# Strassen's scheme for 17 of the 22 weight pairs of the first FFN product

## The chip, the cores and the metric

One core of one Trainium2 chip. The metric is the time of one execution on the device, in microseconds (us); a kernel is run several times and the median is compared. TensorE (PE) multiplies, VectorE (DVE), ScalarE (ACT) and GpSimd (POOL) do elementwise work, SyncE (SP) issues the transfers.

## What is computed

One encoder block on 512 tokens of width 1024 (16 learned meta tokens are put in front for attention). Two attention mixers are merged and added to the stream; then comes the feed-forward part, with which the change has to do:

```python
u = rms_norm(h, pre_ffn_gain[l])
gate_up = u @ w_ffn_in[l]                      # (512, 1024) @ (1024, 2 * 2816)
f = (jax.nn.silu(gate_up[..., :D_FF]) * gate_up[..., D_FF:]) @ w_ffn_out[l]
h = h + rms_norm(f, post_ffn_gain[l])
```

All data are float32. The kernel writes each operand of a product as the sum of a high and a low part in a reduced float32 format (`float32r`) and replaces one product by three: high times high, high times low, low times high.

## The kernel before

Everything is one function, `encoder`. Its stages run one after the other on PE: projections and attention, the merge, the out-projection (`m_out`), normalization and transposition of the tokens (`m_norm`), FFN-in, FFN-out. The order of PE's instructions is the program's order, written by hand and, between out-projection, transposes and FFN-in, by a small planner (`Order`, run in line 1181), in which each piece has a cost and a time at which it is due. The order of the instructions of DVE, ACT, POOL and SP is settled at compile time: roughly, of the instructions whose operands and buffers are available, the one that stands first in the program goes first. On the chip each engine then takes its instructions in that fixed order. Buffers are tiles of pools; all tiles with the same tag share that tag's slots, and a new tile waits until the last reader of an old one is done.

Split (`split`, lines 255 to 261; `sub_hi`, line 252): ACT casts a tile to the high part, DVE subtracts it from the source for the low part. `load_w` (lines 265 to 279) loads 128 x 1024 weights (tag `wr`, three slots), casts them on ACT (line 271) and subtracts on DVE; for the loads number 4 to 51 POOL subtracts three quarters of it (lines 274 to 278, both recorded at line 252). `mm3` (lines 283 to 288) issues the three matmuls.

`m_norm` (lines 1117 to 1153) normalizes the four groups t of 128 tokens, transposes each on PE (line 1147) and splits the result into `uh` and `ul`, 8 blocks of 128 features by 512 tokens (lines 1148 to 1151).

FFN-in (`ffn_in`, lines 1169 to 1179): for each of 22 pairs j of a gate tile and an up tile, 128 output columns each, `proj_g` runs 8 blocks k of `mm3`, first for gate, then for up; ACT takes Silu of gate, DVE multiplies it by up and the product `sg` is split into the hidden tile j (`hid`, tags `xh`, `xl`, `hy0`, `hy1`). The first three pairs run twice, on token columns 0 to 255 and 256 to 511, the other 19 once on all 512 (lines 1110 to 1115):

```python
for c0, c1 in ((0, 256), (256, 512)):
    yield mid.after(("u", c0 // P), ("u", c0 // P + 1), lat=1.5)
    for j in range(NSPLIT):
        yield from ffn_in(j, c0, c1)
for j in range(NSPLIT, NFF):
    yield from ffn_in(j, 0, NTOK)
```

Results of products go to PSUM tiles of `wk_t` (lines 1059 to 1061): four banks in turn.

FFN-out (lines 1187 to 1223) has two halves s of 512 output columns. In each, the weights of two hidden tiles (one c of 11) are loaded at a time and used for four groups of 128 tokens, 24 matmuls of 512 columns; the last two c are loaded ahead into `xw` and run group by group, so that each group's end (lines 1210 to 1223: square sums, gain, the residual, the output's transfer) lies beside the next group's matmuls. The gains (`gb`, three rows, tag `kk`) are loaded at the start of `m_norm`.

Of the kernel before, what the change touches and what calls it, by code (L numbers as in the profile page):

```python
# [236 lines left out]
def encoder(ctx, tc, I, out, dbg=None):  # L237
# [27 lines left out]
    def load_w(src, k=KT, dst=None):  # L265
        raw = wp.tile([P, k, D // k], F32, tag="wr", name="wr", bufs=RB)
        sp.dma_start(out=raw, in_=src.rearrange("p (k c) -> p k c", k=k))
        if dst is None:
            dst = [wp.tile([P, k, D // k], F32R, tag=t, name=t) for t in ("wh", "wl")]
        wh, wl = dst  # L270
        act.copy(out=wh, in_=raw)  # L271

        nw[0] += 1
        cut = 3 * k // 4 if 4 <= nw[0] < 52 else 0
        if cut:
            sub_hi(wl[:, 0:cut], raw[:, 0:cut], wh[:, 0:cut], pool)
        sub_hi(wl[:, cut:], raw[:, cut:], wh[:, cut:])
        return wh, wl
# [42 lines left out]
    rot = const.tile([P, 3, EXT], F32, name="rot")  # L321
    rbc = const.tile([P, EXT], F32, name="rbc")
# [22 lines left out]
    atp = at.__enter__()  # L345
    ps = ctx.enter_context(tc.tile_pool(name="ps", bufs=1, space=PSUM))
# [717 lines left out]
    gb = [zp.tile([P, D], F32, tag="kk", name="gb", bufs=4) for n in range(3)]  # L1064
# [31 lines left out]
    def m_out():  # L1096
        accs[0], accs[1] = [acc_t(), acc_t()], [acc_t(), acc_t()]
        for k in range(KT):
            for t in range(2):
# [4 lines left out]
        for t in (2, 3):
            accs[t] = [wk_t(), wk_t()]
            for k in range(KT):
                out_step(t, k, k == 0, k == KT - 1)
                yield 1.3, 0.0
            mid.flag(("acc", t))
        for c0, c1 in ((0, 256), (256, 512)):  # L1110
            yield mid.after(("u", c0 // P), ("u", c0 // P + 1), lat=1.5)
            for j in range(NSPLIT):
                yield from ffn_in(j, c0, c1)
        for j in range(NSPLIT, NFF):
            yield from ffn_in(j, 0, NTOK)

    def m_norm():
        for t in range(4):
            yield mid.after(("acc", t))
# [7 lines left out]
            for s in range(2):  # L1127
                jk = tl.tile([P, D], BF16, tag="jk", name="jk2", bufs=2)
# [15 lines left out]
            for s in range(2):  # L1144
# [6 lines left out]
                split(uh[:, 4 * s:4 * s + 4, ts], ul[:, 4 * s:4 * s + 4, ts], trv)  # L1151
                yield 0.44, 0.0
# [7 lines left out]
    def hid(c, j):  # L1160
        if j < KT:
            if not hx:
                hx.extend(big.tile([P, KT, NTOK], F32R, tag=n, name="hx") for n in ("xh", "xl"))
            return hx[c][:, j, :]
        if not hy:
            hy.extend(tl.tile([P, NFF - KT, NTOK], F32R, tag="hy%d" % n, name="hy") for n in range(2))
        return hy[c][:, j - KT, :]

    def ffn_in(j, c0, c1):
# [15 lines left out]
    NC = NFF // 2
    NT = 2
    for s in range(2):
        cs = slice(s * 512, (s + 1) * 512)
# [5 lines left out]
        def step(t, c, w):  # L1194
            ts = slice(t * P, (t + 1) * P)
            for k2 in range(2):
                k = 2 * c + k2
                mm3(acc[t], (hid(0, k)[:, ts], hid(1, k)[:, ts]), (w[0][:, k2], w[1][:, k2]),
                    k == 0, k == NFF - 1)

        for c in range(NC - NT):
# [3 lines left out]
        last = [(c, load_w(I["w_fo"][s * NC + c], k=2, dst=(xw[:, 2 * n], xw[:, 2 * n + 1])))
                for n, c in enumerate(range(NC - NT, NC))]
# [102 lines left out]
```

## Time and profile before

| | |
|---|---|
| three runs | 971.58, 974.36, 974.38 us; median 974.36 |
| the profiled execution | 973.73 us, its span 971.9 us |
| mean granted clock of TensorE | 0.997 |
| busy: PE, DVE, ACT, POOL | 955.4, 571.4, 445.8, 287.3 us |
| FFN-in | from 601.39 to 845.14 us of the span |
| FFN-out | from 845.14 us to the end |

Times in rows are from the span's start. Matmuls are pipelined: the recorded duration of one reaches over the start of the next, so the pace is read from the starts. L252 is line 252 of the kernel; helpers' lines stand for all their callers, and the operands' names tell the stage. In brackets stands what ended an engine's idle time. A busy share is an average; what bounds a stage is read from the waits of the engine that is never idle there.

### The profile page before, as it was taken

The numbers are of one execution on the slowest core, as the hardware profiler recorded it, in microseconds if no ns is written. First come the engines' busy times: TensorE is split into PE (matmuls) and PEld (weight loads), VectorE is DVE, ScalarE is ACT, GpSimd is POOL, SyncE is SP. The second block draws the span as 40 slices with busy tenths as digits, with TensorE's granted clock in tenths as the row PEclk, the third lists the DMA queues.
The fourth block names the chain that finished last, engine by engine and source line by source line (L and its number), as shares of the span: only waits on it lengthen the run. The fifth ranks groups of instructions, "written<-read, shape, count | busy, mean of one in ns | idle before, by whom it ended". The sixth has DMA issues, their size and how long they took to land.

```text
span 971.9 us, 14256 instructions
## 1 busy us (share of the span) xinstructions
PE 955.4 (98%) x5307; PEld 825.3 (85%) x5307; DVE 571.4 (59%) x1061; ACT 445.8 (46%) x828; POOL 287.3 (30%) x262
## 2 busy tenths in 40 slices
PE   9899999999999999999999999999999999999997
PEld 9788879888898999989888888988888888888885
DVE  5738888998664768878656838843333334323224
ACT  6327766775644447666645424532222323222221
POOL 0544446543232333233213222644343400000000
PEclk9999999999999999999999999999999999999999
DMA  9383132252425252444432731442323232324122
GB/s 339 125 225 102 40 109 58 71 135 75 112 76 135 77 135 72 132 133 126 114 87 89 240 106 66 155 149 88 109 87 105 90 109 87 109 87 142 53 65 87
DMA packets 37141, 109.34 MB, mean 112 GB/s; under 512 B 6080, under 2 KB 6592, under 8 KB 37072
## 3 DMA queue, kind: packets, MB, share of 16 engines
q1 hardware_dynamic: 37072, 108.43, 36.8%
q8 instruction: 42, 0.69, 0.3%
q14 instruction: 27, 0.22, 0.1%
HBM read 87.04 MB, written 2.10 MB: 92 GB/s over the span
## 4 chain that ended last, share of the span: by engine, by line
PE 86%; DVE 6%; DMA 2%; SPq 2%; issue 1%; ACT 1%; POOL 1%; DVEq 0%; ACTq 0%; POOLq 0%
PE pr L287 18%; PE pr L288 18%; PE pr L286 18%; PE Sd L853 3%; PE wk L287 2%; PE wk L286 2%; PE wk L288 2%; PE Sw L705 2%; PE O L761 2%; PE tr L893 2%; PE tr L286 2%; PE tr L288 2%; PE tr L287 2%; PE tr L754 2%; PE Od L906 2%
## 5 line engine op out<-in xcount | busy, mean ns | idle before, releaser
L252 POOL TENSOR_TENSOR wl<-wr,wh 128x768 fp32r<-128x768 f32 (+1 forms) x76 | 170.8, 2248 | 235.4 <-ACT wh L271 156.5
L286 PE MATMUL pr<-xh,wh 128*128 128x264 f32 (+1 forms) x616 | 200.7, 326 | 0.2 <-ACT xh L392 0.2
L287 PE MATMUL pr<-xl,wh 128*128 128x264 f32 (+1 forms) x616 | 197.1, 320 | 0.7 <-DVE xl L393 0.7
L288 PE MATMUL pr<-xh,wl 128*128 128x264 f32 (+1 forms) x616 | 197.0, 320 | 0.3 <-POOL wl L252 0.3
L271 ACT CAST wh<-wr 128x1024 fp32r<-128x1024 f32 x78 | 81.9, 1051 | 215.5 <-PE pr L287 84.4
L252 DVE TENSOR_TENSOR wl<-wr,wh 128x1024 fp32r<-128x1024 f32 (+2 forms) x110 | 107.5, 978 | 120.2 <-ACT wh L271 108.5
L288 PEld LDWEIGHTS pr<-xh,wl 128*128 128x128 f32 x616 | 116.3, 189 | 9.0 <-POOL wl L252 0.5
L287 PEld LDWEIGHTS pr<-xl,wh 128*128 128x128 f32 x616 | 116.6, 189 | 8.5 <-DVE xl L393 1.1
L286 PEld LDWEIGHTS pr<-xh,wh 128*128 128x128 f32 x616 | 116.5, 189 | 7.8 <-ACT xh L392 0.3
L287 PE MATMUL pr<-ul,wh 128*128 128x512 f32 (+1 forms) x304 | 110.9, 365 | 0.3 <-DVE ul L252 0.3
L286 PE MATMUL pr<-uh,wh 128*128 128x512 f32 (+1 forms) x304 | 111.0, 365 | 0.0
L288 PE MATMUL pr<-uh,wl 128*128 128x512 f32 (+1 forms) x304 | 110.7, 364 | 0.0
L521 ACT CAST wh<-wr 128x1024 fp32r<-128x1024 f32 x56 | 58.5, 1048 | 44.2 <-PE pr L287 29.1
L287 PEld LDWEIGHTS pr<-ul,wh 128*128 128x128 f32 x304 | 57.4, 189 | 9.6 <-DVE ul L252 0.5
L286 PEld LDWEIGHTS pr<-uh,wh 128*128 128x128 f32 x304 | 57.4, 189 | 9.2
L288 PEld LDWEIGHTS pr<-uh,wl 128*128 128x128 f32 x304 | 57.4, 189 | 8.9
L558 POOL TENSOR_TENSOR ta<-ta,tb 128x528 f32<-128x528 f32 (+1 forms) x26 | 36.5, 1404 | 79.8 <-DVE tb L546 53.9
L858 DVE TENSOR_REDUCE nm<-Sd 128x1 f32<-128x528 f32 x64 | 45.1, 705 | 21.1 <-PE Sd L853 20.3
L308 POOL TENSOR_TENSOR r3y<-r3v,mhalf 128x1 f32<-128x1 f32 x4 | 2.2, 548 | 186.9 <-DVE r3v L307 186.9
L719 POOL TENSOR_SCALAR p<-p,rc 128x272 f32<-128x272 f32 (+1 forms) x64 | 36.0, 574 | 47.7 <-DVE rc L717 44.3
L861 ACT ACTIVATE pp<-Sd,nm 128x528 f32<-128x528 f32 x40 | 28.0, 699 | 39.3 <-DVE pa L874 22.6
L853 PE MATMUL Sd<-Kd,Qd 128*128 128x264 f32 x256 | 43.3, 291 | 1.3 <-ACT pp L861 0.7
(377 smaller groups left out, 1991.8 us busy)
## 6 DMA issues: line engine op xcount, KB each, us to landing
wr<-in_w_in_dram SPq DMA_DIRECT2D x50, 512.0 KB, 4.3
wr<-in_w_fi_dram SPq DMA_DIRECT2D x50, 512.0 KB, 3.5
wr<-in_w_fo_dram SPq DMA_DIRECT2D x22, 512.0 KB, 3.5
Kd<-hl SPq DMA_DIRECT2D x32, 132.0 KB, 2.4
Kd<-Kd SPq DMA_DIRECT2D x16, 264.0 KB, 3.7
Q<-hl SPq DMA_DIRECT2D x64, 64.0 KB, 2.0
Qd<-hl SPq DMA_DIRECT2D x64, 64.0 KB, 2.3
wr<-in_w_bs_dram SPq DMA_DIRECT2D x8, 512.0 KB, 4.0
```

The source lines that it names most:

```text
L252: (eng or dve).tensor_tensor(out=lo, in0=src, in1=hi.bitcast(F32), op=ALU.subtract)
L271: act.copy(out=wh, in_=raw)
L286: pe.matmul(out=ps, lhsT=ah, rhs=bh, start=first, stop=False)
L287: pe.matmul(out=ps, lhsT=ah, rhs=bl, start=False, stop=False)
L288: pe.matmul(out=ps, lhsT=al, rhs=bh, start=False, stop=last)
L521: T("ACT", 1.05, lambda: act.copy(out=wh.t, in_=wr.t), r=[wr], w=[wh], prio=pr_)
L558: T("POOL", 0.05 + 1.3 * m, lambda: pool.tensor_tensor(out=ta.t[:, :, 0:n], in0=ta.t[:, :, 0:n], in1=tb.t[:, :, 0:n], op=ALU.add), r=[tb], ...
L705: pe.matmul(out=Sw2[S.slot][:, 0:nk], lhsT=QS[g][hh].t[:, i * P:(i + 1) * P], rhs=KB[g].t[:, x, r0:r1], start=(x == 0), stop=(x == 1))
L719: T("POOL", 0.2 + 0.43 * c, lambda z=z: pool.tensor_scalar(out=pt.t[:, z, 0:nk], in0=pt.t[:, z, 0:nk], scalar1=rc.t[:, z:z + 1], scalar2=1 ...
L853: pe.matmul(out=S.t[:, s, 0:HALF], lhsT=Q[c].t[:, i * P:(i + 1) * P], rhs=K[c].t[:, x, s * HALF:(s + 1) * HALF], start=(x == 0), stop=(x = ...
L858: T("DVE", 0.71, lambda S=S, c=c, one=one: dve.tensor_reduce(out=nm.t[:, c, one], in_=S.t[:, :, 0:HALF], axis=AX.XY, op=ALU.min), r=[S], w ...
L861: T("ACT", 0.9, lambda S=S, c=c, one=one, p=p: act.activation(out=p().rearrange("p (a b) -> p a b", a=2), in_=S.t[:, :, 0:HALF], func=AF.E ...
```

## The change

The first five pairs stay as they were (three on halves of the columns, two on 512). For each of the other 17 the 256 x 1024 block of weights (gate and up) and the 1024 x 512 tokens are taken as 2 x 2 blocks: gate and up by the features' halves (`g1`, `g2`, `u1`, `u2`), features' halves by tokens' halves (`B11`, `B21`, `B12`, `B22`). Strassen's scheme, in the form with fifteen additions, gives the four results with seven products of half size instead of eight. `product` runs one: 4 blocks k of three matmuls on 256 columns. The sums of tokens are made once (`combine`) from unsplit copies of the transposed tokens (`uT`, one more ACT copy for each half of a group in `m_norm`). The sums of weights are made for each pair in `prep`, one pair ahead, in float32 on DVE, and then split. Part of the sums of results is made in PSUM by accumulating products onto one another; the rest needs copies on ACT (`s12`, `up`, `u3`) and adds on DVE. Products 4 and 3 of a pair, with which it ends, are issued among those of the next pair.

The hidden tiles are kept in float32 and split only in the first half of FFN-out (`hid_split`), in an order of the weights (`CS`) that begins with the tiles 16 to 19. POOL takes part in splitting loads 4 to 17 only. The third row of the gains is loaded after FFN-in. To make room, two tables move from a pool that lasts to one that ends with attention, the out-projection's split weights go to other tags (`T`, `sx`, `hr`), `f` and `xw` to `xh` and `xl`.

```diff
-        cut = 3 * k // 4 if 4 <= nw[0] < 52 else 0
+        cut = 3 * k // 4 if 4 <= nw[0] < 18 else 0
...
-        for j in range(NSPLIT, NFF):
+        for j in range(NSPLIT, NPLAIN):
             yield from ffn_in(j, 0, NTOK)
...
                 split(uh[:, 4 * s:4 * s + 4, ts], ul[:, 4 * s:4 * s + 4, ts], trv)
+                if not uT:
+                    uT.extend(zp.tile([P, 4, 256], F32, tag="kk", name="uT", bufs=4) for _ in range(2))
+                if t == 2 and s == 0:
+                    x = big.tile([P, KT, 256], F32, tag="xl", name="uT")
+                    uT.extend([x[:, 0:4], x[:, 4:8]])
+                act.copy(out=uT[s + t // 2 * 2][:, :, t % 2 * P:(t % 2 + 1) * P], in_=trv)
...
     NSPLIT = 3
+    NPLAIN = 5
...
-        dve.tensor_tensor(out=sg, in0=sg, in1=pu, op=ALU.mult)
-        split(hid(0, j)[:, c0:c1], hid(1, j)[:, c0:c1], sg)
+        dve.tensor_tensor(out=hid(j)[:, c0:c1], in0=sg, in1=pu, op=ALU.mult)
 
     mid.run([m_norm(), m_out()])
 
+    TM = tl.tile([P, 4, 2, 4, 256], F32R, tag="T", name="TM")
+    B11, B21, B12, B22 = uT
+
+    def combine(i, x, y, op):
+        t = tl.tile([P, 4, 256], F32, tag="sx", name="tf", bufs=4)
+        dve.tensor_tensor(out=t, in0=x, in1=y, op=op)
+        split(TM[:, i, 0], TM[:, i, 1], t)
+        return t
+
+    t1_ = combine(0, B12, B11, ALU.subtract)
+    t2_ = combine(1, B22, t1_, ALU.subtract)
+    combine(2, B22, B12, ALU.subtract)
+    combine(3, B21, t2_, ALU.subtract)
...
+    RHS = [u_part(0, 0), u_part(1, 0), u_part(1, 1), *((TM[:, i, 0], TM[:, i, 1]) for i in (3, 0, 1, 2))]
+    nx = [0]
+
+    def pair():
+        nx[0] += 1
+        return zp.tile([P, 2, 512], F32R, tag="kk", name="sx", bufs=4) if nx[0] % 2 else two("sx", 4, "sx")
+
+    def prep(j):
+        g = wp.tile([P, KT, P], F32, tag="wr", name="wg", bufs=RB)
+        u = wp.tile([P, KT, P], F32, tag=("wh", "wl")[j % 2], name="wu")
+        for t, n in ((g, j), (u, NFF + j)):
+            sp.dma_start(out=t, in_=I["w_fi"][n].rearrange("p (k c) -> p k c", k=KT))
...
+        gh, gl = (wp.tile([P, D], F32R, tag=t, name=t) for t in ("wh", "wl"))
+        act.copy(out=gh, in_=g)
+        S = zp.tile([P, 4, 512], F32, tag="hl", name="S")
+        g1, g2, u1, u2 = g[:, 0:512], g[:, 512:], u[:, 0:512], u[:, 512:]
+        dve.tensor_tensor(out=S[:, 0], in0=u1, in1=u2, op=ALU.add)
+        dve.tensor_tensor(out=S[:, 1], in0=S[:, 0], in1=g1, op=ALU.subtract)
+        sub_hi(gl, g, gh)
+        dve.tensor_tensor(out=S[:, 2], in0=g1, in1=u1, op=ALU.subtract)
+        dve.tensor_tensor(out=S[:, 3], in0=g2, in1=S[:, 1], op=ALU.subtract)
+        ha, la, uu, hb_, lb = (pair() for _ in range(5))
+        split(ha, la, S[:, 0:2])
+        split(uu[:, 0], uu[:, 1], u2)
+        split(hb_, lb, S[:, 2:4])
...
+    def product(o, n, lhs, first=True):
+        lhs, rhs = [x.rearrange("p (k c) -> p k c", k=4) for x in lhs[n - 1]], RHS[n - 1]
+        for k in range(4):
+            mm3(o, (lhs[0][:, k], lhs[1][:, k]), (rhs[0][:, k], rhs[1][:, k]), first and k == 0, k == 3,
+                skip_group_check=not first)
+
+    def finish(j, w, X_, ZW, s12, up):
+        product(ZW[:, 256:512], 3, w, first=False)
+        sg = tl.tile([P, NTOK], F32, tag="sg", name="sg", bufs=2)
+        dve.tensor_tensor(out=sg, in0=ZW, in1=s12, op=ALU.add)
+        act.activation(out=sg, in_=sg, func=AF.Silu)
+        dve.tensor_tensor(out=hid(j), in0=sg, in1=up, op=ALU.mult)
+
+    prev = None
+    w = prep(NPLAIN)
+    for j in range(NPLAIN, NFF):
+        nw_ = prep(j + 1) if j + 1 < NFF else None
+        X2, ZW = wk_t()[:, 0:256], wk_t()
...
+        product(X2, 1, w)
+        act.copy(out=s12[:, 0:256], in_=X2)
+        product(ZW[:, 0:256], 2, w)
+        if prev:
+            product(prev[2], 4, prev[1], first=False)
+            act.copy(out=prev[5][:, 0:256], in_=prev[2])
+        product(X2, 6, w, first=False)
+        act.copy(out=s12[:, 256:512], in_=X2)
+        product(ZW[:, 256:512], 5, w)
+        if prev:
+            finish(*prev)
+        product(X2, 7, w, first=False)
+        act.copy(out=u3, in_=X2)
+        dve.tensor_tensor(out=up[:, 256:512], in0=ZW[:, 256:512], in1=u3, op=ALU.add)
+        prev = (j, w, X2, ZW, s12, up)
+        w = nw_
+    product(prev[2], 4, prev[1], first=False)
+    act.copy(out=prev[5][:, 0:256], in_=prev[2])
+    finish(*prev)
+
+    gb.append(zp.tile([P, D], F32, tag="kk", name="gb", bufs=4))
+    sp.dma_start(out=gb[2], in_=I["gains"][:, 2])
+    CS = [8, 9, 0, 1, 2, 3, 4, 5, 6, 7, 10]
...
+        split(h, l, hid(k))
+        return h, l
...
-        for c in range(NC - NT):
+        def parts(c):
+            if s == 0:
+                for k in (2 * c, 2 * c + 1):
+                    H[k] = hid_split(k)
+
+        for c in CS[:NC - NT]:
             w = load_w(I["w_fo"][s * NC + c], k=2)
+            parts(c)
             for t in range(4):
                 step(t, c, w)
```

## Rows read from the trace of the kernel before

**Rows 1.** The page: the span, the busy line of all engines, and the shares by engine of the chain that ended last.

```profile
span 971.9 us, 14256 instructions
...
PE 955.4 (98%) x5307; PEld 825.3 (85%) x5307; DVE 571.4 (59%) x1061; ACT 445.8 (46%) x828; POOL 287.3 (30%) x262
...
PE 86%; DVE 6%; DMA 2%; SPq 2%; issue 1%; ACT 1%; POOL 1%; DVEq 0%; ACTq 0%; POOLq 0%
```

**Rows 2.** The table by stage (start:end in us from the span's start; length; busy us of PE, of PE's weight loader, of DVE, ACT and POOL, with counts of instructions in brackets; granted clock of TensorE; DMA share; GB/s). In order: FFN-in on the first 256 token columns, on the second 256, on all 512, FFN-out's first half, its second half.

```profile
601.30:620.40 19.10, 19.10 (x162) 19.00 (x160) 17.23 (x29) 11.76 (x21) 10.30 (x8) 1.00 0.26 84
620.40:638.40 18.00, 17.66 (x147) 17.45 (x146) 10.97 (x14) 8.49 (x13) 13.43 (x7) 1.00 0.63 202
638.40:845.10 206.70, 206.70 (x914) 171.29 (x913) 69.72 (x76) 59.47 (x76) 54.51 (x27) 1.00 0.31 101
845.10:899.40 54.30, 54.30 (x241) 44.98 (x241) 16.56 (x16) 13.66 (x15) 0.00 (x0) 1.00 0.35 115
899.40:956.00 56.60, 56.60 (x252) 46.89 (x251) 11.88 (x14) 10.29 (x14) 0.00 (x0) 1.00 0.16 48
```

**Rows 3.** All waits of PE on other engines from 600 to 956 us (us in total, times, longest).

```profile
PE pr L287 <- DVE ul L252: 0.3, 1, 0.3
```

**Rows 4.** PE in order of time (start us, duration us, line, operation, shape): the second stretch of 256 columns from its first matmul to its last, then the first of 512 columns and the first of FFN-out, with which FFN-in is over.

```profile
620.41 0.39 PE L286 MATMUL pr<-uh,wh 128*128 128x256 f32 x1
621.13 0.39 PE L287 MATMUL pr<-ul,wh 128*128 128x256 f32 x1 [0.34 <-DVE ul L252]
621.36 0.28 PE L288 MATMUL pr<-uh,wl 128*128 128x256 f32 x1
...
638.27 0.28 PE L288 MATMUL wk<-uh,wl 128*128 128x256 f32 x1
638.39 0.40 PE L286 MATMUL pr<-uh,wh 128*128 128x512 f32 x1
...
845.14 0.39 PE L286 MATMUL acc<-wh,hx 128*128 128x512 f32 x1
```

**Rows 5.** Groups of DVE and ACT instructions by line and shape from 790 to 956 us, where POOL does not run (count, busy us, mean ns of one, idle before).

```profile
L252 DVE TENSOR_TENSOR wl<-wr,wh 128x1024 fp32r<-128x1024 f32 x26 | 31.8, 1224 | 63.5 <-ACT wh L271 62.7
...
L252 DVE TENSOR_TENSOR hy<-sg,hy 128x512 fp32r<-128x512 f32 x6 | 4.1, 684 | 0.0
L1178 DVE TENSOR_TENSOR sg<-sg,pr 128x512 f32<-128x512 f32 x3 | 2.1, 687 | 10.2 <-PE pr L288 10.2
...
L271 ACT CAST wh<-wr 128x1024 fp32r<-128x1024 f32 x26 | 27.4, 1053 | 88.8 <-PE acc L288 28.4 <-issue 23.4 <-PE pr L287 19.2
...
L256 ACT CAST hy<-sg 128x512 fp32r<-128x512 f32 x6 | 3.7, 622 | 0.0
L1177 ACT ACTIVATE sg<-pr 128x512 f32<-128x512 f32 x5 | 2.9, 589 | 0.0
```

**Rows 6.** The same from 600 to 850 us, for shapes that the group above does not have, and DVE and POOL where both run.

```profile
L252 DVE TENSOR_TENSOR hx<-sg,hx 128x512 fp32r<-128x512 f32 x5 | 10.6, 2129 | 0.6
...
L252 DVE TENSOR_TENSOR ul<-tr,uh 128x512 fp32r<-128x512 f32 x5 | 3.3, 682 | 0.3 <-ACT uh L256 0.3
...
L1178 DVE TENSOR_TENSOR sg<-sg,pr 128x256 f32<-128x256 f32 x3 | 1.2, 412 | 1.5 <-PE pr L288 1.5
...
L1177 ACT ACTIVATE sg<-pr 128x256 f32<-128x256 f32 x6 | 2.3, 379 | 0.0
L256 ACT CAST uh<-tr 128x512 fp32r<-128x512 f32 x4 | 2.2, 580 | 0.0
...
L252 POOL TENSOR_TENSOR wl<-wr,wh 128x768 fp32r<-128x768 f32 x37 | 77.1, 2084 | 95.0 <-ACT wh L271 95.0
```

**Rows 7.** All engines in order of time around the end of one tile's matmuls: its last matmul and the DVE instruction that reads the result.

```profile
649.08 0.39 PE L288 MATMUL pr<-uh,wl 128*128 128x512 f32 x1
...
649.57 0.69 DVE L1178 TENSOR_TENSOR sg<-sg,pr 128x512 f32<-128x512 f32 x1 [4.18 <-PE pr L288]
```

**Rows 8.** All engines in order of time where the second 256 columns begin: the two casts and the two subtractions that split the last transposed tokens.

```profile
619.78 1.06 ACT L256 CAST uh<-tr 128x512 fp32r<-128x512 f32 x2
...
620.39 1.29 DVE L252 TENSOR_TENSOR ul<-tr,uh 128x512 fp32r<-128x512 f32 x2 [0.33 <-ACT uh L256]
```

**Rows 9.** DMA issues by destination and source: count, KB each, median us from issue to landing.

```profile
wr<-in_w_fi_dram SPq DMA_DIRECT2D x50, 512.0 KB, 3.5
wr<-in_w_fo_dram SPq DMA_DIRECT2D x22, 512.0 KB, 3.5
...
gb<-in_gains_dram SPq DMA_DIRECT2D x3, 512.0 KB, 3.7
```

More of the change, by code (lines that the diff above doesn't have):

```diff
@@ L281, in mm_t, with mm3 @@
         return max(0.109, n / 2400.0 + 0.0135)
-    def mm3(ps, a, b, first, last):
+    def mm3(ps, a, b, first, last, **more):
         ah, al = a
         bh, bl = b
-        pe.matmul(out=ps, lhsT=ah, rhs=bh, start=first, stop=False)
-        pe.matmul(out=ps, lhsT=ah, rhs=bl, start=False, stop=False)
-        pe.matmul(out=ps, lhsT=al, rhs=bh, start=False, stop=last)
+        pe.matmul(out=ps, lhsT=ah, rhs=bh, start=first, stop=False, **more)
+        pe.matmul(out=ps, lhsT=ah, rhs=bl, start=False, stop=False, **more)
+        pe.matmul(out=ps, lhsT=al, rhs=bh, start=False, stop=last, **more)
     def proj_g(ps, w, x, c0, c1):
@@ L1061, in wk_t @@
         return pr_t() if nb["wk"] % 4 else ps.tile([P, 512], F32, tag="av", name="wk")
-    gb = [zp.tile([P, D], F32, tag="kk", name="gb", bufs=4) for n in range(3)]
+    gb = [zp.tile([P, D], F32, tag="kk", name="gb", bufs=4) for n in range(2)]
     xrow = zp.tile([P, 2, D], F32, tag="hl", name="xrow")
@@ L1069, in encoder, with two @@
     U = (uh, ul)
-    wo = [tl.tile([P, KT - 1, 2, 512], F32R, tag="hy%d" % c, name="wo") for c in range(2)]
+    def two(tag, n, name):
+        return tl.tile([P, 2, 512], F32R, tag=tag, name=name, bufs=n)
+    woh = tl.tile([P, 16, 512], F32R, tag="T", name="woh").rearrange("p (k s) c -> p k s c", s=2)
+    wol = [two("sx", 4, "wol") if k < 4 else two("hr", 3, "wol") for k in range(KT - 1)]
+    uT = []
     wts = {}
@@ L1121, in m_norm @@
             if t == 0:
-                for n in range(3):
+                for n in range(2):
                     sp.dma_start(out=gb[n], in_=I["gains"][:, n])
@@ L1151, in m_norm, with hid @@
                 split(uh[:, 4 * s:4 * s + 4, ts], ul[:, 4 * s:4 * s + 4, ts], trv)
+                if not uT:
[4 more added lines that the diff above has]
+                act.copy(out=uT[s + t // 2 * 2][:, :, t % 2 * P:(t % 2 + 1) * P], in_=trv)
                 yield 0.44, 0.0
             mid.flag(("u", t))
-    hx = []
-    hy = []
     NSPLIT = 3
[L1160 to L1167, printed above, removed]
+    NPLAIN = 5
+    hf = {}
+    def hid(j):
+        x = j // KT if j < 2 * KT else 2 + (j - 2 * KT) // 2
+        if x not in hf:
+            hf[x] = (big.tile([P, KT, NTOK], F32, tag=("xh", "xl")[x], name="hid") if x < 2 else
+                     tl.tile([P, 2, 512], F32, tag="hr", name="hid", bufs=3))
+        return hf[x][:, j - KT * x if x < 2 else j % 2, :]
     def ffn_in(j, c0, c1):
@@ new lines, in encoder, with hid_split @@
+    product(prev[2], 4, prev[1], first=False)
[4 more added lines that the diff above has]
+    CS = [8, 9, 0, 1, 2, 3, 4, 5, 6, 7, 10]
+    hs_ = {}
+    def hid_split(k):
+        if k >= 2 * KT:
+            x = k // 2
+            if x not in hs_:
+                hs_[x] = zp.tile([P, 2, 512], F32R, tag="kk", name="hl", bufs=4)
+            y = "A" if x < 10 else "B"
+            if y not in hs_:
+                hs_[y] = zp.tile([P, 4, 512], F32R, tag="hl", name="hh") if y == "A" else two("sx", 4, "hh")
+            h, l = hs_[y][:, k - 16 if y == "A" else k - 20, :], hs_[x][:, k % 2, :]
+        else:
+            x = ("oh", "ol")[k // KT]
+            if x not in hs_:
+                hs_[x] = big.tile([P, KT, 512], F32R, tag=x, name="hl")
+            if "T" not in hs_:
+                hs_["T"] = tl.tile([P, 16, 512], F32R, tag="T", name="hh")
+            h, l = hs_["T"][:, k, :], hs_[x][:, k % KT, :]
+        split(h, l, hid(k))
+        return h, l
@@ L1197, in step @@
                 k = 2 * c + k2
[L1198 to L1201 removed]
+                mm3(acc[t], (H[k][0][:, ts], H[k][1][:, ts]), (w[0][:, k2], w[1][:, k2]),
+                    c == CS[0] and k2 == 0, c == CS[-1] and k2 == 1)
+        def parts(c):
[3 more added lines that the diff above has]
+        for c in CS[:NC - NT]:
             w = load_w(I["w_fo"][s * NC + c], k=2)
+            parts(c)
             for t in range(4):
                 step(t, c, w)
+        xw = big.tile([P, 4, 2, 512], F32R, tag="xl", name="xw")
         last = [(c, load_w(I["w_fo"][s * NC + c], k=2, dst=(xw[:, 2 * n], xw[:, 2 * n + 1])))
[L1206 removed]
+                for n, c in enumerate(CS[NC - NT:])]
+        for c in CS[NC - NT:]:
+            parts(c)
+        if s == 0:
+            f = big.tile([P, 4, D], F32, tag="xh", name="f")
         for t in range(4):
```

24 lines of the change are left out of this document (16 added, 8 removed).

## The prediction

> **What bounds the kernel now.** I read the page's busy shares first, then the stages, then PE's waits, then single instructions. The page shows PE busy 98% of the span and on 86% of the chain that ended last [rows 1]. A busy PE alone proves little, because matmuls overlap, so look at the stages: the first FFN-in stretch on 256 token columns, the second, FFN-in on 512 columns, FFN-out's first and second half [rows 2]. PE is busy for all of each but 0.34 us, at granted clock 1.00, while DVE is busy 34% (69.72 of 206.70), ACT 29% and DMA 31% of the 512-column stage. The list of PE's waits from 600 to 956 us has a single entry, 0.3 us [rows 3]. So in these stages nothing but matmul pace counts, and what is taken from PE comes off the end, as long as the others keep up.
>
> The pace comes from start times, not from durations (390 and 280 ns overlap). On 256 columns, 141 intervals from 621.36 to 638.27 take 16.91 us: 0.1199 us each. On 512 columns, the 19 pairs j=3..21 are 19 x 48 = 912 matmuls from 638.39 to 845.14: 0.2267 us each [rows 4]. The half-width matmul costs 53% of a full one, not 50%.
>
> **The matmuls.** A pair of weight tiles (gate and up) takes 2 tiles x 8 k x 3 = 48 matmuls of 512 columns: 10.88 us. Seven products x 4 k x 3 = 84 matmuls of 256 columns take 10.07 us. The scheme's 12.5% becomes 7.4%: 0.81 us a pair, **13.7 us for 17 pairs**. The rows of 256 columns are the same form as the products (three matmuls for one k, weights reloaded for each, one bank accumulating), so I take their pace.
>
> Here a rule can be weighed. The rows leave 13.3 ns over N/2.4 at either width (0.1199 against 0.1067, 0.2267 against 0.2133), and the change issues 36 more matmuls a pair, which is 0.48 us. The Trainium skill, "TensorE: Matmul & The Clock Gate", section "Back-to-back issue gap", gives a gap of N/2.4 + 2.5 ns; by it the pair would go from 10.36 to 9.17 us and the change would save an estimated 20.2 us. The sum goes by the rows.
>
> **DVE per product pair**, with durations from stretches without POOL, since the new split keeps POOL out there (it ends at the 17th load) [rows 5, 6]: four sums and differences of the weights at 0.684, three low parts of 1024 at 1.224, one of 512 at 0.684, the sum of ZW and s12 and the product with up at 0.687 each, the half-width add of up at 0.412. Together 2.74 + 3.67 + 0.68 + 1.37 + 0.41 = 8.9 us in 10.07. **ACT**: three 1024 casts at 1.053, one of 512 at 0.622, four 256-column copies out of PSUM at 0.379 (nearest row: Silu of that shape), Silu 0.589: 5.9 us. **DMA**: two 512 KB loads a pair as before, 3.5 us to land [rows 9], three and two deep in buffers. Neither engine is the bound, but DVE goes from a third to 88%, and its cover is 1.2 us a pair. At +13% per instruction it is gone, at +22% (8.9 to 10.88) so is the whole gain.
>
> **The waits it adds.** Products run 1, 2, 4 of the pair before, 6, 5, 3 of the pair before, 7, starting at 0, 1.44, 2.88, 4.32, 5.76, 7.20, 8.64. A reader starts 0.27 us after the last matmul's slot (649.08 + 0.227 to 649.57 [rows 7]).
> - X2 is copied out after 1, 6 and 7, and two products lie between each copy and the next write: 2.88 us for 0.27 + 0.38 and at most one 1.05 cast ahead on ACT. Hidden.
> - ZW must be added out after the pair before's product 3 (end 8.64) and before the next pair's product 2 overwrites that bank at 11.51. The add can start at 8.91 and needs 0.69, so 1.9 us are left for whatever stands before it in DVE's queue. Queued behind it: silu on ACT, the product, then the next sums.
> - The pair's weight buffers (four and four) come back after product 5 (ha, la) and after the pair before's product 3 (hb, lb). The next low parts can be written from 7.5 on and are needed by product 6 at 14.4. Hidden.
> - At the end nothing lies between product 7 and product 4 of the last pair: matmul end to reader 0.27, copy 0.38, wake of PE 0.06 (ul ends 620.39 + 0.68 = 621.07, PE at 621.13 [rows 4, 6, 8]): **+0.7 us**, bounds 0.5 and 1.1.
>
> **Before the products.** The results of the first pairs are no longer split in FFN-in, which takes contended 2.13 us DVE instructions away [rows 6], and POOL's part of the loads goes to DVE at 1.22; PE waits for neither now. Eight more ACT copies of transposed tiles (0.58) stand behind the casts at line 1148-1151. The second 256-column stretch already begins with a late ul: 0.72 instead of 0.12 between its first two matmuls [rows 4, 8]. It waits for the first half only, whose cast comes ahead of the new copy. I take 0, bounds -0.6 and +0.6. The four combinations (4 x 2 x 1.22 = 9.8 us DVE) and the first pair's preparation (7.1) with ten loads (12.3) and the products (2.6) make 31.8 us of DVE in the 39 us from 621 to 660. Hidden.
>
> **FFN-out's start.** 22 splits, 0.622 ACT and 0.684 DVE each, make 13.7 and 15.0 us in a half of 54.3 us where ACT has 13.66 and DVE 16.56 [rows 2, 5]. The first step needs the splits of tiles 16 and 17; their buffers come free in the last pair, 4 us or more ahead of use. If that cover failed: one load and two splits, about 2 us. On SP's queue the third row of gains now waits for a buffer of the last pairs, with the first loads of FFN-out behind it: freed 6.5 us before FFN-in ends, against 0.7 to issue, 3.5 to land, 1.05 and 1.22, at worst 0.3 late. I take 0, bound 1.5. Memory moved from one pool to another costs nothing: the out-projection's weights are loaded as before.
>
> **Sum.** -13.7 + 0.7 = -13.0 us. The profiled execution took 973.73 us (span 971.9), 0.6 below the median of 974.36; against the median that is **961.4 us**.
>
> **Rivals.**
> 1. *ZW late, slower.* Preparation of the next pair is written ahead of the add in the program, so DVE's queue could hold la, uu's low part and lb (3.13 us) before it. Then ZW comes out at 8.91 + 3.13 + 0.69 = 12.73 and PE waits 1.25 us a pair, 16 times: 20 us, **981 us**. It decides from 0.81 us a pair on. For it: the 1.9 us are few, DVE is at 88%, and a queue once set isn't changed. Against: lb or la can run from 7.5 on, before the add is ready.
> 2. *Half of it.* Only la and lb stand ahead (2.45): 0.6 us a pair, **971 us**; one of them in every other pair gives 964 to 967.
> 3. *DVE becomes the bound, no change.* 22% longer instructions give **974 us**. For it: rows of 684 ns instructions that took 2129 [rows 6]. Against: in those POOL was at work, and here it isn't.
> 4. *The fixed 13.3 ns vanish.* Then a pair goes from 48 x 0.2133 to 84 x 0.1067, saves 1.28, and the run takes **953 us**. Against: 141 and 912 intervals show the 13.3 at both widths. The gap in the Trainium skill's page on TensorE named above comes near this case, with an estimate of 955 us; the trace does not agree with it.
> 5. *The products don't get cheaper.* On 256 columns the weight loader is busy 19.00 of 19.10 us, on 512 columns 83% [rows 2]; if it set the pace and products loaded slower, the gain would go at 0.1295 a matmul: **975 us**. Against: 0.1199 was reached with the loader just as busy.
>
> **Chances.** Forecast (959.5 to 964) 0.73, rival 1 0.08, rival 2 0.10, rival 3 0.04, rival 4 0.02, rival 5 0.03. About 0.3%, or 2.9 us, is what a measurement of this kernel can tell from no change: its three runs spread over 2.8. Faster: forecast, 2 and 4, 0.85. Same: 3 and 5 with small rests, 0.07. Slower: 0.08. The range goes from 958.5 (the late ul gone, runs like the fastest of before) to 968, which takes in the late FFN-out start and most of rival 2.
>
> **What would show it.** Right: starts 0.12 apart through all products, FFN-out's first matmul near 832 us in place of 845.14, one PE gap of about 0.7 us before the last pair's product 4, PE's waits otherwise empty, DVE at 80 to 88% and POOL idle through the products, FFN-out's first half as long as before. Wrong: a PE wait for the add of ZW or for a low part in every pair, DVE instructions of 512 elements well over 0.69 us, or a PE gap of 2 us where FFN-out begins.

## The result and the profile after

| | before | after | ratio, 95% interval |
|---|---|---|---|
| first comparison, medians | 974.13 us | 963.96 us | 0.9902 [0.9874, 0.993] |
| second (`after_again`) | 973.49 us | 962.59 us | 0.9889 [0.9872, 0.9906] |
| third (`after_third`) | 973.62 us | 962.51 us | 0.9884 [0.9869, 0.9899] |
| the profiled execution, span | 971.9 us | 963.5 us | |
| FFN-in, first matmul to FFN-out's first | 243.75 us | 231.54 us | |

The change is faster by 10.2 to 11.1 us; 13.0 were forecast. The page of after shows the trade: PE has 612 more instructions and 12.0 us less busy time than in [rows 1], DVE goes from 59% to 70% of the span, POOL from 30% to 22%.

```profile
span 963.5 us, 15670 instructions
...
PE 943.4 (98%) x5919; PEld 844.1 (88%) x5919; DVE 670.3 (70%) x1202; ACT 504.3 (52%) x939; POOL 216.2 (22%) x228
...
PE 88%; DVE 5%; DMA 2%; ACT 1%; SPq 1%; issue 1%; DVEq 0%; ACTq 0%
```

The table by stage of after, with the columns of [rows 2]; here the 512-column stage is cut in two, plain pairs 3 and 4 and then the 17 product pairs, and the last line runs to the end of the span. FFN-out is cut here near the true end of its first half; the 54.30 us stretch of [rows 2] ends before it, with 241 of the half's 264 matmuls:

```profile
604.60:623.50 18.90, 18.90 (x160) 18.86 (x159) 17.51 (x28) 13.86 (x24) 7.67 (x5) 1.00 0.35 107
623.50:641.60 18.10, 17.66 (x147) 17.45 (x146) 17.09 (x18) 11.47 (x15) 0.00 (x0) 1.00 0.52 169
641.60:663.39 21.79, 21.79 (x98) 18.04 (x97) 10.49 (x14) 6.66 (x8) 0.00 (x0) 1.00 0.50 161
663.39:836.17 172.78, 171.86 (x1429) 171.45 (x1428) 138.25 (x185) 98.31 (x158) 0.00 (x0) 1.00 0.35 108
836.17:896.00 59.83, 59.83 (x266) 49.55 (x265) 27.56 (x38) 21.97 (x34) 0.00 (x0) 1.00 0.29 97
896.00:963.50 67.50, 60.04 (x265) 49.37 (x264) 20.58 (x38) 11.66 (x18) 2.19 (x4) 0.96 0.20 71
```

Seventeen product pairs take 172.78 us, where 17 pairs of 48 matmuls at [rows 4]'s 0.2267 took 184.99: 12.21 less. The waits of PE over FFN-in take the place of the single one in [rows 3] (us in total, times, longest):

```profile
PE pr L286 <- ACT u L1272: 0.5, 1, 0.5
PE pr L286 <- ACT s L1261: 0.5, 1, 0.5
PE pr L288 <- DVE wl L252: 0.4, 1, 0.4
```

The third stands in the second 256-column stretch and takes the place of the late ul; that stretch and the one ahead of it are as long as before (36.98 against 37.00 us). The other two are in PE's order of time (start, duration): the first pair's products 2 and 6, the last pair's 7 and 4, and FFN-out's first matmul.

```profile
666.15 0.28 PE L288 MATMUL pr<-uh,wl 128*128 128x256 f32 x1
666.88 0.39 PE L286 MATMUL pr<-TM,sx 128*128 128x256 f32 x1 [0.46 <-ACT s L1261]
667.11 0.28 PE L287 MATMUL pr<-TM,sx 128*128 128x256 f32 x1
...
832.45 0.28 PE L288 MATMUL pr<-TM,sx 128*128 128x256 f32 x1
833.20 0.39 PE L286 MATMUL pr<-TM,sx 128*128 128x256 f32 x1 [0.46 <-ACT u L1272]
833.42 0.28 PE L287 MATMUL pr<-TM,sx 128*128 128x256 f32 x1
...
836.17 0.40 PE L286 MATMUL acc<-wh,hh 128*128 128x512 f32 x1
```

Read them by starts: 0.73 and 0.75 us where 0.12 is the pace, and the matmul behind comes after 0.22 or 0.23 and not 0.12. Each wait costs 0.72 us or a little more, not the 0.46 that the list names. Then 17 x 84 x 0.1199 = 171.22, and 171.22 + 0.72 + 0.73 = 172.67 of the 172.78 measured.

**Why the first pair waits** is read from ACT's queue in the same stretch. Product 1 ends near 665.0; its copy (L1261) would run then, but two casts for the next pair's weights stand ahead:

```profile
664.99 1.05 ACT L256 CAST sx<-S 128x1024 fp32r<-128x1024 f32 x1 [0.53 <-DVE S L1228]
665.95 0.61 ACT L256 CAST sx<-wu 128x512 fp32r<-128x512 f32 x1
666.47 0.36 ACT L1261 COPY s<-pr 128x256 f32<-128x256 f32 x1
```

In every later pair products 2 and 4 lie between 1 and 6; the first pair has no pair before it, so only product 2 does.

### The profile page after: what moved, and what is told of

Its sections match the earlier page's. It is cut to its first block, busy times and chain, and to the rows that moved or that the text cites. A ratio compares the mean times of both kernels' runs of the same rounds, so it can differ in the third digit from the quotient of the medians.

```text
span 963.5 us, 15670 instructions
## 1 busy us (share of the span) xinstructions
PE 943.4 (98%) x5919; PEld 844.1 (88%) x5919; DVE 670.3 (70%) x1202; ACT 504.3 (52%) x939; POOL 216.2 (22%) x228
## 4 chain that ended last, share of the span: by engine, by line
PE 88%; DVE 5%; DMA 2%; ACT 1%; SPq 1%; issue 1%; DVEq 0%; ACTq 0%
PE pr L286 19%; PE pr L287 19%; PE pr L288 19%; PE Sd L853 3%; PE wk L287 2%; PE wk L288 2%; PE wk L286 2%; PE Sw L705 2%; PE O L761 2%; PE tr L893 2%; PE Od L906 2%; PE tr L288 2%; PE tr L287 2%; PE tr L286 2%; PE tr L754 2%; PE acc L288 1%
## 5 line engine op out<-in xcount | busy, mean ns | idle before, releaser
L252 POOL TENSOR_TENSOR wl<-wr,wh 128x1024 fp32r<-128x1024 f32 (+2 forms) x42 | 99.8, 2377 | 141.3 <-ACT wh L521 78.0
L252 DVE TENSOR_TENSOR wl<-wr,wh 128x1024 fp32r<-128x1024 f32 (+2 forms) x76 | 91.5, 1208 | 53.5 <-ACT wh L271 43.7
L521 ACT CAST wh<-wr 128x1024 fp32r<-128x1024 f32 x56 | 58.5, 1049 | 42.1 <-PE pr L287 34.5
L271 ACT CAST wh<-wr 128x1024 fp32r<-128x1024 f32 x44 | 46.2, 1052 | 65.3 <-PE pr L288 17.9
L286 PE MATMUL pr<-TM,sx 128*128 128x256 f32 x240 | 68.1, 284 | 0.9 <-ACT u L1272 0.5
L287 PE MATMUL pr<-TM,sx 128*128 128x256 f32 x240 | 67.9, 283 | 0.0
L288 PE MATMUL pr<-TM,sx 128*128 128x256 f32 x240 | 67.9, 283 | 0.0
L288 PE MATMUL pr<-uh,wl 128*128 128x256 f32 (+1 forms) x200 | 59.2, 296 | 0.4 <-DVE wl L252 0.4
L286 PE MATMUL pr<-uh,wh 128*128 128x256 f32 (+1 forms) x200 | 59.3, 296 | 0.0
L287 PE MATMUL pr<-ul,wh 128*128 128x256 f32 (+1 forms) x200 | 59.1, 296 | 0.0
L252 DVE TENSOR_TENSOR sx<-S,sx 128x1024 fp32r<-128x1024 f32 x34 | 41.6, 1225 | 25.1 <-PE wk L287 12.7
L256 ACT CAST sx<-S 128x1024 fp32r<-128x1024 f32 x34 | 35.7, 1050 | 25.8 <-PE pr L288 8.1
## 6 DMA issues: line engine op xcount, KB each, us to landing
Kd<-hl SPq DMA_DIRECT2D x32, 132.0 KB, 2.4
```

Of the source, the lines that this page charges most:

```text
L252: (eng or dve).tensor_tensor(out=lo, in0=src, in1=hi.bitcast(F32), op=ALU.subtract)
L256: act.copy(out=hi, in_=src)
L286: pe.matmul(out=ps, lhsT=ah, rhs=bh, start=first, stop=False, **more)
L287: pe.matmul(out=ps, lhsT=ah, rhs=bl, start=False, stop=False, **more)
L288: pe.matmul(out=ps, lhsT=al, rhs=bh, start=False, stop=last, **more)
L521: T("ACT", 1.05, lambda: act.copy(out=wh.t, in_=wr.t), r=[wr], w=[wh], prio=pr_)
```

## The experiments

**Where the other 3 us of the first profile went.** FFN-in starts at 604.63 us after, at 601.39 before, while the stages from there to the end are 11.6 us shorter. Four kernels on one chip.

`before_again` is the kernel before, unedited.

> The kernel before, unchanged, once more, for a second profile of the stages ahead of the changed one. In its first profile the first FFN product starts at 601.4 us, in the profile of the changed kernel at 604.6 us, though every engine's instructions stand in the same order up to 515 us. Theory A (the two profiled executions differ by themselves, whichever kernel it is): the median stays at 971 to 975 us, and the start of the first FFN product can fall anywhere from 601 to 605 us in this profile. Theory B (the change delays the early stages): it starts within 1 us of 601.4 us again.

973.28 us, ratio 0.9993 [0.9984, 1.0002]; FFN-in started at 602.1. `before_moved` moves two tables and nothing else:

```
-    rot = const.tile([P, 3, EXT], F32, name="rot")
-    rbc = const.tile([P, EXT], F32, name="rbc")
...
+    rot = atp.tile([P, 3, EXT], F32, name="rot")
+    rbc = atp.tile([P, EXT], F32, name="rbc")
```

> The kernel before with one part of the change alone: the two tables rot and rbc are allocated in the attention stage's pool and not in the constants', so every tile behind them lies elsewhere in SBUF, as in the changed kernel; no instruction is added or removed. Theory A (the 3.2 us by which the first FFN product started later in the changed kernel's profile differ between executions): ratio 1.000 to the kernel before, within 0.2%. Theory B (the place of the tiles in SBUF costs the 3.2 us): 974 + 3 = 977 us, ratio 1.003, and the first FFN product starts near 604.6 us.

973.98 us, ratio 1.0003 [0.9993, 1.0012]; FFN-in started at 603.5. `after_again` is the changed kernel.

> The changed kernel once more. Theory A (early stages differ by execution): the median is 974.1 less the 12.2 us by which its stages from the first FFN product's start to its end were shorter in the profiles, plus 0.6 us of the longer end, that is 962.5, ratio 0.988; over the fastest executions of both the difference is 9 to 12 us too. Theory B (the change costs 3 us before the products): 962.5 + 3.2 = 965.7, ratio 0.991, and the first FFN product starts at 604.6 us in this profile again.

962.59 us; FFN-in started at 601.9, 2.7 us earlier than in the same kernel's first profile, and took 231.1 us. The first pair's gap was 0.31 in place of 0.73, a loss of 0.3 with the next matmul's.

Much of what moves the start is seen in the early windows of the first profile after (first two fences) and of `before_again` (the other two): 35 to 40, 70 to 75 and 75 to 80 us, columns as in the stage table, and then the group of the 128 matmuls that follow (min/median/max ns, first and last start).

```profile
35.00:40.00 5.00, 2.69 (x14) 1.87 (x14) 4.97 (x8) 2.36 (x5) 4.10 (x4) 1.00 0.03 10
...
70.00:75.00 5.00, 2.55 (x11) 1.72 (x10) 0.69 (x1) 1.67 (x2) 2.37 (x1) 1.00 0.91 273
75.00:80.00 5.00, 3.72 (x15) 3.20 (x16) 1.98 (x9) 2.23 (x9) 0.50 (x2) 0.78 0.40 124
```

```profile
L705 PE MATMUL Sw<-KK,Q x128: 282/343/535, 76.3 to 208.6; 128*128 128x272 f32 x64, 128*128 128x400 f32 x64
```

```profile
35.00:40.00 5.00, 3.03 (x12) 2.29 (x13) 4.96 (x7) 2.29 (x4) 4.10 (x4) 0.83 0.00 0
...
70.00:75.00 5.00, 3.59 (x17) 2.61 (x15) 0.69 (x1) 1.68 (x2) 2.37 (x1) 1.00 0.72 207
75.00:80.00 5.00, 5.00 (x26) 4.41 (x27) 3.66 (x15) 3.88 (x13) 1.48 (x4) 1.00 0.28 105
```

```profile
L705 PE MATMUL Sw<-KK,Q x128: 282/342/451, 75.0 to 205.7; 128*128 128x272 f32 x64, 128*128 128x400 f32 x64
```

In both, PE is idle for about 2 us between 35 and 40. In `before_again` TensorE's mean granted clock is 0.83 there (a mix of its levels 1.2 and 2.4 GHz) and 0.82 in the next 5 us; in the first profile after it stays at 1.00. PE then reaches the transfer of Q 1.0 us earlier, waits 3.7 us for it in place of 1.4 (Q also comes 1.3 us later here), and the clock falls behind that wait, to 0.78: the 128 matmuls take 132.3 us from first to last start in place of 130.7.

Call profiles in which the clock falls between 35 and 45 us the first kind, those in which it stays at 1.00 the second. In the second kind PE reaches Q at 71.9 to 72.6 us and the 128 matmuls take 132.0 to 132.3; in the first kind at 73.2 or later and 130.6 to 130.7. When Q comes differs within both (the first of the 128 starts between 74.5 and 76.3). All three profiles of before are of the first kind. Of the eleven of the changed kernel and its variants four are of the second (`after`, `last_order`, `eight_pairs`, `eighteen`). So the moved tables do not cost 3.2 us (the interval of `before_moved` ends at 1.2), and executions of the same kernel do differ ahead of FFN-in, by 2.7 us in the changed kernel (604.6 and 601.9).

`after_third` is the changed kernel once more, to see what is left.

> The changed kernel a third time, beside the three below. By its stages it saves 12.0 us from the first FFN product's first matmul to the end (370.5 against 358.5 us in the profiles), by the medians of the runs so far 10.2 and 10.9 us. Theory A (the rest is the mix of early stages that the executions happen to have): the product's start falls between 601 and 605 us, and the time is that start plus 360.3 to 360.7. Theory B (the change itself moves the early stages by 1 to 2 us): the median difference stays at 10 to 11 us and the start lies on average a microsecond or more behind the 601.2 us that the median of before stands for (973.5 less 372.3).

962.51 us, profiled execution 963.32 with a start of 602.7: 360.6 behind it, as expected. In before that distance is 372.3 in two profiles (973.73 - 601.39, 974.41 - 602.1). So from FFN-in on the change gives 11.7 to 12.0 us. The medians differ by only 10.2 to 11.1.

All executions on record together show where the rest is. Take 372.3 us from the time of each of the 74 executions of before and `before_moved`, and from each of the 12 of the changed kernel the 360.3 to 360.6 us of its own profile. As an estimate from these distances, FFN-in starts at 601.0 us on average before and never later than 603.5; in the changed kernel it starts at 602.7 on average, and three times at 604.6 to 605.1. So the change does cost some 1.7 us ahead of FFN-in (95% interval 0.7 to 2.7), as Theory B has it. The moved tables alone don't account for it (the 11 executions of `before_moved` give 601.4). The second kind, some 1.5 us dearer in the 128 matmuls, would make up about 0.5 of it at its share of four profiles in eleven. The rest, and what in the change brings it on, isn't shown.

**What a pair is worth.** `eight_pairs` sets one constant: `NPLAIN = 14` for 5.

> The changed kernel with 8 of the 22 pairs by seven products in place of 17; the other 14 are done as before. Theory A (each pair is worth the twelve fewer matmul slots, 0.81 us, and nothing else in the stage costs time): the first FFN product, from its first to FFN-out's first matmul, takes 231.3 + 9 x 0.81 = 238.6 us, a product pair takes 10.07 us and a plain pair 10.88 us, and the time is 7.3 us above the changed kernel's. Theory B (part of the 12.2 us gained is a fixed gain or loss, as of the plain pairs that no longer prepare a second operand of the result): the stage takes 2 us or more away from 238.6.

968.05 us, ratio 0.9956 [0.9941, 0.9972]. FFN-in took 238.0 us with only the last pair's wait in it. From before's 243.75, 8 x 0.8075 - 0.73 = 5.73 gives 238.0 (0.8075 us is 48 x 0.2267 less 84 x 0.11993); `after_again` has 17 x 0.8075 - 0.73 - 0.3 = 12.7, which gives 231.0 of 231.1. Theory A, with the waits at their full price.

**The add of ZW made late (rival 1).** In `add_late` the add is made to follow the low part of the pair after it:

```
+    low_b = []
...
-        split(hb_, lb, S[:, 2:4])
+        act.copy(out=hb_, in_=S[:, 2:4])
+        low_b.append(dve.tensor_tensor(out=lb, in0=S[:, 2:4], in1=hb_.bitcast(F32), op=ALU.subtract))
...
-        dve.tensor_tensor(out=sg, in0=ZW, in1=s12, op=ALU.add)
+        add = dve.tensor_tensor(out=sg, in0=ZW, in1=s12, op=ALU.add)
+        if j < NFF - 2:
+            behind(add, low_b[-1:])
```

> The changed kernel with the order of two VectorE instructions swapped in 16 pairs: the add that empties the gate tile's PSUM sums (419 ns) is held behind the 1225 ns subtraction of the next pair's low parts, which otherwise follows it. That is the first rival of the prediction made true (the add late by one subtraction of the weights' preparation), at its smallest step. Theory A (the add came 1.6 us ahead of the next pair's product 2, which writes that tile, so 1.2 us of delay are nearly covered): 0 to 0.35 us a pair, 0 to 6 us in all. Theory B (the order of VectorE's queue has no slack there, and the delay falls on TensorE whole): 1.2 us a pair, 19 us in all.

968.89 us; FFN-in 237.7, some 6.3 over the changed kernel's, 0.39 us a pair: a little beyond the upper end of Theory A (6 us, 0.35 a pair), far from Theory B. (The add takes 0.684 us; the 419 ns in the expectation is the half-width add's.) DVE's queue in the changed kernel, one pair:

```profile
740.27 0.68 DVE L252 TENSOR_TENSOR sx<-wu,sx 128x512 fp32r<-128x512 f32 x1
740.87 0.68 DVE L1248 TENSOR_TENSOR sg<-pr,s 128x512 f32<-128x512 f32 x1
741.62 1.23 DVE L252 TENSOR_TENSOR sx<-S,sx 128x1024 fp32r<-128x1024 f32 x1
...
745.89 1.23 DVE L252 TENSOR_TENSOR wl<-wg,wh 128x1024 fp32r<-128x1024 f32 x1 [0.31 <-ACT wh L1224]
747.04 0.68 DVE L1231 TENSOR_TENSOR S<-wg,S 128x512 f32<-128x512 f32 x1
749.20 1.23 DVE L252 TENSOR_TENSOR sx<-S,sx 128x1024 fp32r<-128x1024 f32 x1 [1.48 <-PE pr L287]
```

and in `add_late`, DVE first, then PE where product 1 ends and product 2 begins:

```profile
710.46 1.23 DVE L1238 TENSOR_TENSOR sx<-S,sx 128x1024 fp32r<-128x1024 f32 x1 [0.67 <-ACT sx L1237]
711.60 0.68 DVE L1251 TENSOR_TENSOR sg<-wk,s 128x512 f32<-128x512 f32 x1
```

```profile
712.01 0.28 PE L288 MATMUL pr<-uh,wl 128*128 128x256 f32 x1
712.43 0.36 PE L286 MATMUL wk<-uh,wh 128*128 128x256 f32 x1
712.63 0.28 PE L287 MATMUL wk<-ul,wh 128*128 128x256 f32 x1
```

In the changed kernel the add (740.87) is over 1.7 us before product 2, which starts two products after 740.41, at 743.29. In `add_late` it ends at 712.28, 0.15 us behind the 712.13 at which product 2 would start; the price is 0.30 at that matmul and 0.08 at the next. The bracket names no wait, and the list of waits shows only two entries for the add, of 1.0 us together. A producer that is 0.15 us late costs 0.38.

**How much VectorE has to spare.** `dve_plus3` and `dve_plus6` do a subtraction, whose result stays the same, four and seven times over. The edit of the first:

```
-        dve.tensor_tensor(out=S[:, 2], in0=g1, in1=u1, op=ALU.subtract)
+        for _ in range(4):
+            dve.tensor_tensor(out=S[:, 2], in0=g1, in1=u1, op=ALU.subtract)
```

> The changed kernel with one 128x512 subtraction of weights done four times over in each pair's preparation, which adds 3 x 0.60 = 1.8 us a pair to VectorE, 9.9 us by its busy time of 8.13 us a pair. Theory A (VectorE has 10.07 - 8.13 = 1.9 us to spare and waits for nothing else on TensorE's path): no change beyond 0.1 us a pair, 0 to 2 us in all. Theory B (the prediction's own 8.9 us of VectorE work a pair, 1.2 us to spare): 10.7 us a pair, 0.6 us over TensorE's, 10 us slower in all.

969.73 us; FFN-in 237.8, 6.4 over the changed kernel's, on average 0.4 us a pair (1 us of it at the last pair). Neither end: 1.8 us more cost 0.4, so on average some 1.4 were free. Busy time (8.13 of 10.07) overstated the cover, the prediction's sum of durations (8.9) understated it. The 1.4 lies close to the longest idle time in DVE's queue above, 1.48 us ahead of 749.20, where it waits for a weight buffer that PE lets go; the 0.31 is behind another engine's cast. That it is this idle time which was filled is not shown, though: the compiled queue also has another order, and the price isn't even. From the ninth pair on it falls on every second pair, and in the pair between DVE is idle for 1.1 us, waiting for ACT's cast of a weight sum. Two pairs in a row:

```profile
752.74:762.82 10.08, 10.08 (x87) 10.08 (x86) 8.97 (x13) 5.27 (x9) 0.00 (x0) 1.00 0.35 106
762.82:773.74 10.92, 10.33 (x86) 10.12 (x85) 10.79 (x17) 5.48 (x9) 0.00 (x0) 1.00 0.32 96
```

> The same subtraction seven times over, 6 x 0.60 = 3.6 us more a pair. Theory A (8.13 + 3.6 = 11.7 us a pair, VectorE is the bound): a pair takes 11.7 us, 1.65 us more than TensorE's 10.07, 26 us slower in all. Theory B (8.9 + 3.6 = 12.5): 2.4 us a pair, 39 us. If the time does not change, VectorE's queue runs ahead of TensorE by more than one pair and the cover is larger than its idle time.

1008.57 us; FFN-in 276.9, some 45.5 more, beyond both. The waits of PE and one of DVE's in the product stage, then two of its stretches:

```profile
PE pr L288 <- DVE sx L252: 26.7, 23, 1.7
PE pr L286 <- ACT sx L256: 2.2, 3, 1.2
PE pr L286 <- ACT u L1273: 1.1, 1, 1.1
```

```profile
DVE sg L1249 <- PE pr L288: 7.8, 7, 1.6
```

```profile
740.00:780.00 40.00, 34.59 (x263) 33.17 (x262) 37.01 (x53) 17.78 (x28) 0.00 (x0) 0.96 0.31 89
...
860.00:879.00 19.00, 15.32 (x104) 14.62 (x102) 14.46 (x21) 10.21 (x19) 0.00 (x0) 0.82 0.33 112
```

DVE is busy 92 to 96% of the stretches from 680 to 860 us and still not the whole bound: PE waits for a low part, so product 3 is late, so DVE's next add waits for PE at the head of its own queue. Each wait costs some 0.26 us more than its listed length (0.72 for 0.46 above), and the granted clock falls to 0.96 in some stretches and to 0.82 in the last.

**The two ends, and more pairs.** `last_order` moves the last pair's product 5 behind its product 7.

> The changed kernel, with the last pair's product 5 issued behind its product 7 in place of ahead of it, so that one product of 1.44 us lies between product 7 and product 4, which share a PSUM tile with a copy by ScalarE between them. Theory A (the 0.75 us between those two products in the profile is the price of the copy, of which 0.12 is the usual pitch): the gap falls to 0.12, product 4 follows product 5 without a wait, and the time is 0.6 us below the changed kernel's. Theory B (the wait moves to the copy behind product 4 or to the add of the last gate tile, which then end the stage): no change in time.

961.97 us against `after_again`'s 962.59, too close to tell. In the profile product 4 no longer waits, but product 3 does, 0.32 us over the pace, for the add of up that reads its bank and needs product 5: half the gain, Theory B's mechanism with another add. `both_ends2` mends both ends otherwise: product 1 of the first pair half-way through the last plain pair, and

```
-    product(prev[2], 4, prev[1], first=False)
-    act.copy(out=prev[5][:, 0:256], in_=prev[2])
+    M4 = wk_t()[:, 0:256]
+    product(M4, 4, prev[1])
+    dve.tensor_tensor(out=prev[5][:, 0:256], in0=M4, in1=u3, op=ALU.add)
```

> The changed kernel with both ends of the seven-product loop mended: product 1 of the first pair is issued half-way through the last plain pair's second tile, so that ScalarE's copy behind it is done before product 6 of that pair; and product 4 of the last pair goes into a PSUM tile of its own, which VectorE adds to the copy that is there already, so that it waits for no copy. Theory A (the two waits cost 0.6 us each and nothing is late behind them): the stage from the first FFN product to FFN-out takes 230.5 us, 0.6 below the 231.1 of a profile where only the last wait fell, and 1.1 below the 231.5 with both. Theory B (the next instruction in line is late in their place, as the add was when product 5 was moved behind product 7): 231.1 or more.

FFN-in took 230.1 us, 1.4 below `after`'s: Theory A and some more, since each mended wait is worth 0.72. The only wait of PE left in it is

```profile
PE pr L288 <- DVE wl L252: 0.4, 1, 0.4
```

Its median, 961.78 us (ratio to before 0.9877 [0.9857, 0.9896]), can't be told from `after_third`'s, measured beside it.

> The same with 18 pairs in place of 17: pair 4 of the weights too is done by seven products, and one plain pair is left between the column halves and the products. Theory A (a pair is worth 0.8 us and the preparation of the first two pairs still fits ahead of them, VectorE having 13 us of idle time between 636 and 653 us in the changed kernel): 229.7 us in the stage, 0.8 below the same kernel with 17 pairs. Theory B (the first pair's second weight tile lands late, since its buffer is let go only by the last plain pair's preparation): a wait of 1 us or more ahead of the first product, no gain.

964.61 us (ratio to before 0.9899 [0.9883, 0.9916]). FFN-in took 232.4 us, Theory B: in the first product the low part of the weights is late, at PE

```profile
648.20 0.28 PE L287 MATMUL pr<-ul,wh 128*128 128x256 f32 x1
650.99 0.39 PE L288 MATMUL pr<-uh,wl 128*128 128x256 f32 x1 [2.50 <-DVE wl L252]
```

DVE's queue holds that low part behind the first preparation's sums, and these wait until 647.2 for the up tile (idle 6.58 us, first line), whose load is issued at 640.55, only after the last plain weights are split (638.92 + 1.23):

```profile
647.18 0.69 DVE L1239 TENSOR_TENSOR S<-wu 128x512 f32<-128x512 f32 x1 [6.58 <-DMA wu<-in_w_fi_dram]
...
649.72 1.22 DVE L252 TENSOR_TENSOR wl<-wg,wh 128x1024 fp32r<-128x1024 f32 x1
```

> The changed kernel with 19 pairs by seven products: no plain pair lies between the column halves and the products, the ends as in the changed kernel. Theory A (0.8 us a pair, the cover is enough): 1.6 us below the changed kernel's stage, 229.5 to 229.9 us. Theory B (the preparation of the first pair, 8 us of VectorE work behind a transfer of 3.5 us, has no plain pair to hide behind): TensorE waits 2 to 8 us at the first product, and the stage takes 231 to 238 us.

FFN-in took 229.8 us, Theory A: 0.2 us of waiting for a low part in the first pair, the last pair's 0.5 as in the changed kernel. Its median is 959.99 us (ratio to before 0.987 [0.9848, 0.9892]), the lowest of all; from FFN-in's start to the end it takes 356.9 us, the changed kernel 358.4 to 358.9, before 370.5. By its stages it is shorter than either, and its median is 2.5 us under `after_third`'s, though the intervals of the two overlap. Nineteen pairs with the mended last end weren't tried.

## Why the prediction was right, step by step

- *The matmuls, -13.7.* Right. `both_ends2`, where no product waits, runs the 17 x 84 products and half a plain tile from 657.51 to 831.60; without the 2.72 us of the latter that is 0.1200 us a matmul, 0.1199 forecast. The rival by which the fixed 13.3 ns vanish is out, and so is the one by which products load slower. The Trainium skill, "TensorE: Matmul & The Clock Gate", section "Back-to-back issue gap", gives its N/2.4 + 2.5 ns as the gap of a matmul by itself; these products, each matmul with its own weight load, don't show it: 0.1200 - 0.1067 leaves 13.3 ns.
- *The wait at the end, +0.7.* Right: 0.63 to the late matmul and 0.10 to the next.
- *X2's copies: "two products lie between each copy and the next write".* Failed for the first pair, where product 4 of a pair before does not exist: 0.3 to 0.7 us. The condition that hid it ("at most one 1.05 cast ahead") fell too, since two casts stood ahead.
- *ZW.* The 1.9 us were 1.7 (741.55 to 743.29). Rival 1 did not happen: the add stands ahead of the low part that follows it. `add_late` shows the margin to be real and thin: one subtraction more, with the cast that it waits for, is 6 us.
- *VectorE.* Durations were as in [rows 5] (684, 1225, 685 ns), the sum was too large: back to back they start 0.60 us apart (743.70, 744.30, 744.90), 0.08 less than they last. Busy 8.13 a pair, 80%, not 8.9 and 88%. What was usable was 1.4 us on average, 1.2 forecast.
- *Before the products, 0.* Right from FFN-in's start on: 36.98 against 37.00 us. *FFN-out's start, 0.* Right: no wait of PE there, and the first half takes 59.87 us against 59.84, from its first matmul to the second half's. (The 54.3 us that the prediction calls a half is the short stretch of [rows 2].)
- *Not foreseen:* 0.3 to 0.6 us behind FFN-out's start (127.1 to 127.3 us from there to the end of the span, 126.7 before). Most of it, 0.44 us, lies behind the last transfer of results, in the program's closing instructions (1.52 us against 1.08); why they take longer wasn't followed.
- *The stages ahead of FFN-in: no term.* The prediction's only word on them is that memory moved from one pool to another costs nothing. The executions give some 1.7 us there, with the cause open. The sign "FFN-out's first matmul near 832 us" thus read 836.17: FFN-in itself began 3.2 us later in that execution, and the first pair's wait came on top.

The sum: -13.7 + 0.73 + 0.3 to 0.7, and 0.3 to 0.6 at the end, makes 11.7 to 12.4 us, against 11.7 to 12.0 measured from FFN-in on. The rest of the way to the medians' 10.2 to 11.1 lies ahead of FFN-in. In the FFN the mechanism was right. That the medians (962.5 to 964.0) still fell into 959.5 to 964 is in part luck: the terms left out all go one way, and in the first comparison they used up the margin. The chance of 0.85 for faster stood on a pace measured at the same width, and this held.

## What to carry to other kernels

Take the pace of a new shape from start times of the same shape in the same kernel: seven eighths of the columns became 92.6% of the time, and that figure was there before the change. For an ordered queue don't take the idle share as free: here 1.9 us of a pair were idle, and on average a little over two thirds of it could be used (`dve_plus3`). Look apart at the first and last pass of a pipelined loop, where the neighbours that hide a wait are missing.

## What the hardware showed that was not expected

- A matmul whose operand or bank is only 0.15 us late costs 0.38 us: its successor too starts late, and neither shows as a wait (`add_late`). A listed wait of 0.46 costs 0.73.
- A faster early stage can lose its gain: with the clock at 1.00 from 35 to 45 us PE got to Q's transfer 1.0 us earlier, waited 3.7 us in place of 1.4, and the clock fell behind that wait; the 128 matmuls that follow took 1.6 us longer. Three other profiles show the same.
